# Strassen's seven products for the value half of an MLP up-projection, in a two-layer encoder kernel on one core

## The chip, the cores and the metric

The kernel runs on one core of a Trainium2 chip. The metric is device time in microseconds (us), from the program's start to its end on that core; lower is better. Three runs of the kernel before gave 2897.88, 2903.08 and 2912.84 us, a median of 2903.08 us.

## The reference, cut to what matters

Two layers over 640 tokens: 512 of a prompt and 8 requests of 16 new tokens each. All data is float32. A layer ends with a gated MLP, whose gate half goes through a causal convolution of width 3 (per sequence):

```python
x = x + jnp.sum(g * proj, axis=2) @ w_out
u = _rms(x, norm_ffn_g) @ ffn_w_up              # 1024 -> 2 * 2816
a_up, v_up = u[..., :D_FF], u[..., D_FF:]       # gate half, value half
ext = jnp.concatenate([conv0.astype(a_up.dtype), a_up], axis=1)
c = ffn_conv_b + sum(ext[:, j:j + T] * ffn_conv_w[j] for j in range(CONV_W))
x = x + (jax.nn.silu(c) * v_up) @ ffn_w_down    # 2816 -> 1024
```

## The kernel before, in words

Everything is one program of some 48,500 instructions. A framework places the instructions on the engines' queues: it goes by the order of the source, but lets an instruction pass an earlier one of its engine that isn't ready yet in its own model of time. The order on each queue is then fixed; on the chip each queue runs strictly in that order and waits where an operand or a buffer isn't there. A buffer belongs to a tag with so many copies (`wh`: 3, `wl`: 3, `mm`: 2, `sc`: 3, ...); a new tile of a tag waits until the users of the oldest one are done.

TensorE multiplies in the format fp32r, which keeps less than float32. So each matrix is split into a high part (a cast on ACT, line 98, in `split`) and a low part, the rest (a subtraction on DVE, line 99), and each product is three matmuls: high by high, high by low, low by high. `wload` brings a weight block from DRAM into `wr` and splits it into `wh` and `wl`.

The stages of a layer: the attention and recurrence branches with their gates; the mix of the branches (lines 1120 to 1149); the output projection with the residual (line 1160 on); the up-projection with the gated activation (lines 1193 to 1249); the down-projection (lines 1274 to 1300).

**Output projection.** Four units of 256 columns, in each five token tiles of 128. In the last unit (`u == 3`) `norm_tile(t - LAG)` is called two tiles later: squares on ACT, the root on POOL (line 127), scaling on DVE (line 144), four transposes per half on TensorE, then the split of the transposed tile into high and low (lines 98, 99, 151, 153). Its result is `xh`, `xl`: the normalised activations, features by tokens.

**Up-projection.** Eleven units `u` of 256 of the 2816 columns. A unit first does the gate half: two blocks of 128 columns times two halves of the 640 tokens (`HT` = 320), each a group of 8 x 3 = 24 matmuls of 320 columns into one PSUM bank `mm` (`projB`, matmuls at line 123). ACT copies the sums out (lines 1206 to 1209), DVE does the convolution (lines 1220 to 1222), ACT the tanh (line 1226), DVE the product that makes it SiLU (line 1227). Then the value half: again four groups of 24, into the banks `sc`, and DVE multiplies them with the gate (lines 1244 to 1247) into `mid`, which stays in SBUF. So a unit has 96 + 96 matmuls.

**Down-projection.** For each half `s` of the 1024 output columns, eleven steps `kp` take two blocks of `mid`, split them on ACT and DVE into `hl` (five buffers `ob`), split a weight block, and run 2 x 3 matmuls of 512 columns for each of the five token tiles (`down`, lines 1270 to 1272). The last three steps are kept back (`late`), so that the token tiles end one after the other.

Of the kernel before, what the change touches and what calls it, by code (L numbers as in the profile page):

```python
# [18 lines left out]
D = 1024  # L19
SEQ = 512  # L20
NB = 8
NS = 16
# [8 lines left out]
class Cols:  # L31
    """tiles [128, n], one a block, read as one [128, k, n]."""
# [21 lines left out]
def body(ctx: ExitStack, tc: tile.TileContext, i, o, depth=DEPTH):  # L54
    nc = tc.nc
    V, A, G, PE, SY = nc.vector, nc.scalar, nc.gpsimd, nc.tensor, nc.sync
    pool = ctx.enter_context(tc.tile_pool(name="sb", bufs=1))
    pp = ctx.enter_context(tc.tile_pool(name="ps", bufs=1, space=PSUM))
    dp = ctx.enter_context(tc.tile_pool(name="dr", bufs=1, space=DRAM))
    BUFS = {  # L60
# [3 lines left out]
    }  # L64
    BUFS.update(TUNE)
    cnt = [0]

    def T(tag, shape, dt=F32, bufs=None):
        cnt[0] += 1
        return pool.tile(shape, dt, tag=tag, bufs=bufs or BUFS[tag], name=f"{tag}_{cnt[0]}")  # L70

    def P(tag, shape=(128, 512)):
        cnt[0] += 1
        return pp.tile(list(shape), F32, tag=tag, bufs=BUFS[tag], name=f"{tag}_{cnt[0]}")

    def C(name, shape, dt=F32, bufs=1):
        cnt[0] += 1
        return pool.tile(shape, dt, tag=name, bufs=bufs, name=f"{name}_{cnt[0]}")
# [50 lines left out]
    def norm_T(xs, gsrc, xh, xl, stag="st"):  # L129
        """rms of token-major halves xs[h] [128, NT, 512] -> split transposed xh, xl, each [128, 4, TOK] x2; a tile a call."""  # L130
# [30 lines left out]
    def projB(w, c0, xh, xl, evac, tag="mm", hs=(0, 1)):  # L161
        """feature-major: columns c0..c0+128 of the unit, all tokens in two halves."""
# [21 lines left out]
    def tok_out(l, t, name, ap_fn):  # L184
        """DMA a token tile: prompt rows or sample rows."""

    def constants():
# [16 lines left out]
        Sbd = []  # L204
        for k in range(4):
            s_ = C(f"Sbd{k}", [128, 128])
            G.memset(s_[:], 0.0)
            Sbd.append(s_)

        qz = []  # L210
        for c in range(2):
            z_ = C(f"qz{c}", [128, 2, TOK])
            G.memset(z_[:], 0.0)
            qz.append(z_)

        # hgrn lower bound: softmax over depth, running sum less the first
# [27 lines left out]
        return masks, rope, hsel, bsel, half2, identf, Sbd, qz, lbs, lb1  # L244

    wz0 = []
    for l in range(depth):
# [15 lines left out]
        # ---- input norm  # L263
# [36 lines left out]
        def scaled_rstd(v, n, rs):  # L300
            """rstd of v / rs^2 over 64, times 1 / rs (rs in its first n columns, the next n are scratch)."""
# [41 lines left out]
        def stream_a():  # L343
# [48 lines left out]
            def a_latents(t):  # L392
# [13 lines left out]
                # rotary key  # L406
# [7 lines left out]
                # queries  # L414
# [19 lines left out]
            for t in range(NT):  # L434
# [5 lines left out]
                for hf in range(2):  # L440
# [21 lines left out]
                    else:  # L462
# [4 lines left out]
                        for bq in range(2):  # L467
                            # rows: high, low, high
# [26 lines left out]
            # == A keys and values  # L495
# [48 lines left out]
            # == A prompt attention  # L544
# [28 lines left out]
            # == A sample requests, against the latent rows  # L573
# [81 lines left out]
        # ---- branch C: differential attention  # L655
        def stream_c():
# [21 lines left out]
            def c_inproj(u):  # L678
                """queries and keys of two blocks; high and low parts of the prompt's go to DRAM."""
# [44 lines left out]
            def c_stack(blk, hh):  # L724
                """a head's two queries and keys as 96 rows: high, low, high against high, high, low."""
# [11 lines left out]
            # == C prompt attention  # L737
# [4 lines left out]
            def p_probs(un, q):  # L742
                """a head's weights for a block of queries, over the first softmax's scale."""
# [59 lines left out]
            # == C sample requests  # L803
# [69 lines left out]
            for bh in range(2):  # L873
# [8 lines left out]
                # each row holds two heads' values; its own half counts  # L882
# [22 lines left out]
        # ---- branch B: gated recurrence  # L905
        def stream_b():
            ob = kept["ob"] = T("ob", [128, 4, TOK])
            late = None
            for u in range(2):
# [39 lines left out]
                for c in range(2):  # L949
# [5 lines left out]
                    # == B diagonal and levels  # L955
# [18 lines left out]
                    # qz holds each head's q (zero in the other head's rows) with its decay from the start of its block, k that to the end of its block, F a block's whole decay  # L974
# [32 lines left out]
                    # == B chunks  # L1007
# [45 lines left out]
                    # == B sample states  # L1053
# [30 lines left out]
        # the branches and gates are traced interleaved, each string's letter advancing its own  # L1084
# [3 lines left out]
        if l == 0:  # L1088
            masks, rope, hsel, bsel, half2, identf, Sbd, qz, lbs, lb1 = constants()
# [20 lines left out]
        ob = kept["ob"]  # L1110

        # == mix: branch projections under their gates
# [38 lines left out]
        # ---- output projection and residual  # L1151
        x2 = [T("ob", [128, NT, 512]) for _ in range(2)]
        for h in range(2):
            if l == 0:
                SY.dma_start(x2[h][:, 0:4], i["x_prompt"][0, :, h * 512:(h + 1) * 512].rearrange("(t p) d -> p t d", p=128))
# [227 lines left out]
```

## Time and profile before

| | |
|---|---|
| median of three runs | 2903.08 us (2897.88 to 2912.84) |
| the profiled execution: first to last instruction (its span) | 2904.4 us |
| its own time as a run | not given apart; the span is 1.3 us above the median and inside the range of the runs |
| TensorE matmuls busy | 2835.3 us, 98% of the span, 19,600 matmuls |
| DVE, ACT, POOL busy | 1472.6, 987.4 and 352.5 us |
| data moved | 293.66 MB, 101 GB/s in the mean |
| stretch of the up-projection in layer 0 and in layer 1 | about 980 to 1304 us, about 2433 to 2738 us |

A matmul's own duration in this profile overlaps with the next one's, so the step from one start to the next is what a matmul costs. "Idle before" an instruction is charged to what came last of the things it waited for.

### The profile page before, as it was taken

To read this page: it belongs to the slowest core of one execution; us is meant where nothing else is said; L and a number is where in the kernel's file an instruction comes from. 1 tells how busy PE (TensorE), PEld (TensorE's weight loads), DVE (VectorE), ACT (ScalarE), POOL (GpSimd) and SP (SyncE) were. 2 spreads that over 40 slices of the span, in tenths; PEclk is the share of its full clock that TensorE was granted. 3 is DMA by queue.
4 is the path that set the end of the run, shared out by engine and by line. 5 is a ranking of instruction groups with operands and counts; after the bars stand their busy time and mean duration, and the time that the engine had idled before them with its cause. 6 is when DMAs were issued, how large, how long until landed. Compare 5 with 4: busy or idle time off the path is not lost. (4 is left out here: it accounts for less than half of the span.)

```text
span 2904.4 us, 48551 instructions
## 1 busy us (share of the span) xinstructions
PE 2835.3 (98%) x19600; PEld 2542.7 (88%) x19600; DVE 1472.6 (51%) x3117; ACT 987.4 (34%) x2074; POOL 352.5 (12%) x559
## 2 busy tenths in 40 slices
PE   7999999999999999999999999999999999999998
PEld 7979997778889999998899799977788899999976
DVE  5465464355565544443454654633646545444444
ACT  4444453232221322222444443623222223222332
POOL 1000120012122001000000011200222210110000
PEclk9999999999999999999999999999999999999999
DMA  4213563322244222222333136443232442222222
GB/s 147 69 50 110 169 173 115 118 89 82 80 140 155 74 73 73 73 85 76 98 110 93 41 120 184 122 141 116 82 98 66 154 134 70 73 77 81 86 73 73
DMA packets 297996, 293.66 MB, mean 101 GB/s; under 512 B 51493, under 2 KB 254765, under 8 KB 296237
## 3 DMA queue, kind: packets, MB, share of 16 engines
q1 hardware_dynamic: 290092, 277.97, 31.1%
q0 software_dynamic: 7680, 12.59, 1.8%
q8 instruction: 155, 2.54, 0.4%
q14 instruction: 69, 0.56, 0.1%
HBM read 245.37 MB, written 44.09 MB: 100 GB/s over the span
## 5 line engine op out<-in xcount | busy, mean ns | idle before, releaser
L99 DVE TENSOR_TENSOR wl<-wr,wh 128x1024 fp32r<-128x1024 f32 (+2 forms) x292 | 370.6, 1270 | 339.1 <-ACT wh L98 336.3
L98 ACT CAST wh<-wr 128x1024 fp32r<-128x1024 f32 (+2 forms) x292 | 305.1, 1045 | 605.9 <-PE sc L123 213.0
L123 PE MATMUL mm<-xh,wh 128*128 128x320 f32 x1280 | 409.0, 320 | 0.0
L123 PE MATMUL mm<-xl,wh 128*128 128x320 f32 x1280 | 408.1, 319 | 0.0
L123 PE MATMUL mm<-xh,wl 128*128 128x320 f32 x1280 | 405.2, 317 | 0.0
L123 PE MATMUL sc<-ob,wh 128*128 128x320 f32 x1568 | 400.6, 310 | 2.9 <-DVE pd L1142 2.9
L123 PE MATMUL mm<-wh,xh 128*128 128x256 f32 (+1 forms) x960 | 281.2, 293 | 6.6 <-ACT xh L1148 3.9
L123 PE MATMUL mm<-wh,xl 128*128 128x256 f32 (+1 forms) x960 | 280.4, 292 | 1.1 <-DVE xl L99 1.0
L123 PE MATMUL mm<-wl,xh 128*128 128x256 f32 (+1 forms) x960 | 280.8, 293 | 0.0
L123 PEld LDWEIGHTS sc<-ob,wh 128*128 128x128 f32 x1568 | 275.1, 188 | 3.7 <-DVE pd L1142 3.7
L123 PE MATMUL mm<-ob,wh 128*128 128x320 f32 (+1 forms) x1088 | 275.1, 312 | 1.2 <-ACT ob L98 0.6
L123 PE MATMUL sc<-ob,wl 128*128 128x320 f32 x832 | 257.6, 310 | 0.0
L123 PEld LDWEIGHTS mm<-xh,wh 128*128 128x128 f32 x1280 | 243.0, 190 | 7.2 <-issue 3.1
L123 PEld LDWEIGHTS mm<-xh,wl 128*128 128x128 f32 x1280 | 242.6, 190 | 6.3 <-issue 3.4
L123 PEld LDWEIGHTS mm<-xl,wh 128*128 128x128 f32 x1280 | 242.9, 190 | 4.9 <-issue 0.4
L123 PE MATMUL mm<-ob,wl 128*128 128x320 f32 (+1 forms) x720 | 224.7, 312 | 0.0
L123 PE MATMUL sc<-pd,wh 128*128 128x320 f32 x608 | 189.3, 311 | 3.4 <-DVE pd L1142 3.4
L123 PEld LDWEIGHTS mm<-wh,xh 128*128 128x128 f32 x960 | 184.1, 192 | 9.3 <-ACT xh L1148 4.3
L123 PEld LDWEIGHTS mm<-ob,wh 128*128 128x128 f32 x1088 | 189.4, 188 | 2.9 <-DVE ob L99 1.1
L123 PEld LDWEIGHTS mm<-wh,xl 128*128 128x128 f32 x960 | 183.8, 192 | 1.7 <-DVE xl L99 1.2
L123 PEld LDWEIGHTS mm<-wl,xh 128*128 128x128 f32 x960 | 184.1, 192 | 1.1 <-issue 0.8
L123 PEld LDWEIGHTS sc<-ob,wl 128*128 128x128 f32 x832 | 156.2, 188 | 0.0
(379 smaller groups left out, 5218.3 us busy)
## 6 DMA issues: line engine op xcount, KB each, us to landing
wr<-in_w_in_dram SPq DMA_DIRECT2D x104, 512.0 KB, 4.2
wr<-in_ffn_w_up_dram SPq DMA_DIRECT2D x88, 512.0 KB, 3.6
wr<-in_ffn_w_down_dram SPq DMA_DIRECT2D x44, 512.0 KB, 3.6
pd<-in_cache_diff_k_dram SPq DMA_DIRECT2D x64, 256.0 KB, 3.8
pd<-in_cache_diff_v_dram SPq DMA_DIRECT2D x64, 256.0 KB, 3.2
gp<-g SPq DMA_DIRECT2D x48, 320.0 KB, 3.8
pd<-gp SPq DMA_DIRECT2D x48, 320.0 KB, 3.8
wr<-in_w_branch_dram SPq DMA_DIRECT2D x24, 512.0 KB, 3.6
```

What stands on the lines that cost most here:

```text
L98: a = A.copy(hi, src)
L99: v = V.tensor_tensor(lo, src, hi.bitcast(F32), op=ALU.subtract)
L123: PE.matmul(out, lhsT=a, rhs=b, start=(j == 0), stop=(j == n - 1))
```

## The change

**SBUF by stage.** Before, one pool holds all tiles. After, a small fixed pool keeps `xh`, `xl`, `wr`, `wh`, `wl` and small things, and each stage opens pools of its own on the left or right side of SBUF and closes them at its end; a tile that lands on the bytes of an earlier stage's tile waits for the users of that tile alone. The scratch of the branches (`qz`, `Sbd` and others) is cleared again in each layer.

**Residual.** `x2`, the residual, is loaded ahead of the mix, written to DRAM tile by tile in the last unit of the output projection, and read back at the start of the down-projection (2 x 1280 KB).

**Activations.** `norm_tile` splits each transposed tile into `aq` (four quadrants: two halves of the tokens by two halves of the features) and also copies it whole into `raw`. `norm_sums` then forms the four sums of quadrants that Strassen's scheme needs and splits them into `S`.

**Value half.** Four products of quadrants (96 matmuls) are replaced by seven products of 4 x 3 = 12 matmuls of 320 columns, 84 in all. Weight sums are made on DVE in the raw block and split as before. Sums that several outputs share stay in a PSUM bank, in which the next product goes on accumulating; three of them are copied to SBUF by ACT and added to another bank by DVE.

**Order.** The gate groups of unit `u + 1` are written between the products of unit `u`.

**Gate.** As before, 96 matmuls; the halving of SiLU is folded into the convolution's weights.

**Gated activations.** Each block goes to DRAM (`midp`, 22 x 320 KB a layer) and comes back twice in the down-projection, once for each `s` (11 x 640 KB each time). `hl` has three buffers in place of five.

The diff, cut to its core:

```diff
+        mr = Phase("mr", "right", aq=4, wr8=2, wh2=2, wl2=2, cw=1, cvo=1, rows=1)
+        nr = Phase("nr", "right", raw=1, e=2, t=2)
...
+    def wslot(shape):
+        wring[0] += 1
+        more = "2" if wring[0] % 5 > 2 else ""
+        return T("wh" + more, shape, F32R), T("wl" + more, shape, F32R)
+    def st_weights(src, c0):
+        w = src.rearrange("(k p) n -> p k n", p=128)
+        raw = T("wr8", [128, 8, 256])
+        for u in range(2):
+            SY.dma_start(raw[:, 4 * u:4 * u + 4], w[:, 4 * u:4 * u + 4, c0:c0 + 256])
...
+        b1h, b1l = wslot([128, 8, 128])
+        split(b1h[:], b1l[:], raw[:, :, 0:128])
+        b2h, b2l = wslot([128, 4, 128])
+        split(b2h[:], b2l[:], b(1, 1))
+        V.tensor_tensor(b(0, 0), b(0, 1), b(0, 0), op=ALU.subtract)
+        V.tensor_tensor(b(0, 1), b(1, 1), b(0, 1), op=ALU.subtract)
+        V.tensor_tensor(b(1, 1), b(1, 1), b(0, 0), op=ALU.subtract)
+        V.tensor_tensor(b(1, 0), b(1, 0), b(1, 1), op=ALU.subtract)
+        t0h, t0l = wslot([128, 4, 256])
+        split(t0h[:], t0l[:], raw[:, 0:4])
+        t1h, t1l = wslot([128, 4, 256])
+        split(t1h[:], t1l[:], raw[:, 4:8])
...
+        def prod(j):
+            z = {1: "X", 6: "X", 7: "X", 4: "X", 5: "Y", 3: "Y", 2: "Z"}[j]
+            first = j in (1, 5, 2)
+            if first:
+                bank[z] = P({"X": "sc", "Y": "tp", "Z": "sc"}[z])[:, :HT]
...
+            prs = [pr for k in range(sh.shape[1]) for pr in ((th[:, k], sh[:, k]), (th[:, k], sl[:, k]), (tl[:, k], sh[:, k]))]
+            for q, (a, b) in enumerate(prs):
+                PE.matmul(ps, lhsT=a, rhs=b, start=first and q == 0, stop=q == len(prs) - 1, skip_group_check=not first)
+            if j in (1, 5, 6):
+                kept_[j] = copy_of(ps)
+            elif j == 2:
+                out(0, 0, kept_[1], ps)
+            elif j == 3:
+                out(0, 1, kept_[6], ps)
+            elif j == 7:
+                out(1, 1, kept_[5], ps)
+            else:
+                out(1, 0, None, ps)
...
+        def norm_sums(c0, c1, S):
+            def r(h, u):
+                return raw[:, 4 * u:4 * u + 4, h * HT + c0:h * HT + c1]
+            V.tensor_tensor(r(1, 1), r(1, 0), r(1, 1), op=ALU.add)
+            G.tensor_tensor(r(1, 0), r(0, 0), r(1, 0), op=ALU.subtract)
+            split(S[0][:, 0, :, c0:c1], S[0][:, 1, :, c0:c1], r(1, 1))
+            V.tensor_tensor(r(0, 0), r(1, 1), r(0, 0), op=ALU.subtract)
+            V.tensor_tensor(r(0, 1), r(0, 1), r(0, 0), op=ALU.subtract)
+            split(S[1][:, 0, :, c0:c1], S[1][:, 1, :, c0:c1], r(0, 0))
+            split(S[3][:, 0, :, c0:c1], S[3][:, 1, :, c0:c1], r(0, 1))
+            split(S[2][:, 0, :, c0:c1], S[2][:, 1, :, c0:c1], r(1, 0))
...
+        norm_tile(3)
+        norm_sums(0, 512 - HT, S)
+        norm_tile(4)
+        norm_sums(512 - HT, HT, S)
...
+            def out(h, c, s, ps):
+                v = ps
+                if s is not None:
+                    v = T("m", [128, HT])
+                    V.tensor_tensor(v[:], s, ps, op=ALU.add)
...
+        ops = {1: plain[0], 2: plain[1], 3: sums[3], 4: plain[3], 5: sums[0], 6: sums[1], 7: sums[2]}
...
+        for u in range(NU):
+            gates = gate_unit(u + 1, ccs[u + 1]) if u + 1 < NU else iter(())
+            value = value_unit(u, ccs[u], wv)
+            for step in (1, 5, 2, 6, 3, 0, 7, 0, 4, 0, 0):
+                if step:
+                    value(step)
+                else:
+                    next(gates, None)
+                if step == 6 and u + 1 < NU:
+                    wv = st_weights(up, FF + (u + 1) * 256)
...
-                hl = T("ob", [128, 4, TOK], F32R)
+                hl = T("hl2" if (11 * s + kp) % 3 else "hl", [128, 4, TOK], F32R)
+                mid = T("pd" if s or kp else "m0", [128, 2, TOK])
+                SY.dma_start(mid[:], midp[kp])
```

In the value loop a `0` stands for one gate group of 24 matmuls of the next unit. The gate half's weights use `wh` and `wl` too (two tiles a unit); `wslot` gives three of five tiles of the value half to `wh` and two of five to the new `wh2`. The value outputs use `m` (2 buffers), the copies `s` (4).

## Rows read from the trace of the kernel before

**Rows 1.** The page: its head and part 1 (busy us, share, instructions).

```profile
span 2904.4 us, 48551 instructions
...
PE 2835.3 (98%) x19600; PEld 2542.7 (88%) x19600; DVE 1472.6 (51%) x3117; ACT 987.4 (34%) x2074; POOL 352.5 (12%) x559
```

**Rows 2.** Stretches: up-projection of layer 1, down-projection of layer 0 (columns head it).

```profile
core 0: us, PE busy (x) PEld busy (x) DVE busy (x) ACT busy (x) POOL busy (x), PEclk, DMA share, GB/s
2433.00:2738.00 305.00, 305.00 (x2077) 305.00 (x2076) 140.94 (x201) 80.67 (x134) 30.82 (x84) 1.00 0.24 75
1304.00:1453.00 149.00, 149.00 (x647) 119.46 (x646) 66.92 (x85) 54.49 (x83) 1.10 (x2) 1.00 0.27 85
```

**Rows 3.** The chain that ended last: one gate and one value half of 21.

```profile
2512.24 14.12 PE mm L123 x96
2526.36 14.12 PE sc L123 x96
```

**Rows 4.** Groups by line, 2445 to 2730 us: busy us, mean ns, idle before.

```profile
L99 DVE TENSOR_TENSOR wl<-wr,wh 128x1024 fp32r<-128x1024 f32 x40 | 49.0, 1224 | 23.3 <-ACT wh L98 22.5
L98 ACT CAST wh<-wr 128x1024 fp32r<-128x1024 f32 x40 | 42.1, 1053 | 81.6 <-PE sc L123 69.9 <-issue 11.7
L1222 DVE SCALAR_TENSOR_TENSOR a<-e,pd,a 128x656 f32<-128x656 f32 x21 | 18.8, 896 | 0.4
...
L1227 DVE SCALAR_TENSOR_TENSOR a<-e,a 128x656 f32<-128x656 f32 x20 | 16.8, 839 | 8.2 <-ACT e L1226 8.2
...
L1220 DVE TENSOR_SCALAR a<-e,pd 128x656 f32<-128x656 f32 x20 | 12.7, 636 | 89.8 <-POOL pd L1223 89.8
...
L1244 DVE SCALAR_TENSOR_TENSOR pd<-a,sc 128x320 f32<-128x320 f32 x5 | 2.4, 479 | 6.0 <-PE sc L123 6.0
...
L1246 DVE SCALAR_TENSOR_TENSOR pd<-a,sc 128x192 f32<-128x192 f32 x4 | 1.4, 352 | 0.4 <-PE sc L123 0.4
L1247 DVE SCALAR_TENSOR_TENSOR pd<-a,sc 128x128 f32<-128x128 f32 x4 | 1.1, 280 | 0.0
```

**Rows 5.** Groups by line, one shape each, whole span: nearest shapes on DVE.

```profile
L95 DVE COPY a<-tp 128x512 f32<-128x512 f32 x62 | 42.7, 689 | 66.2 <-PE tp L831 46.3 <-PE tp L857 13.6 <-PE tp L562 5.1
...
L99 DVE TENSOR_TENSOR ob<-xh,ob 128x640 fp32r<-128x640 f32 x32 | 25.0, 818 | 3.8 <-ACT ob L98 3.8
...
L99 DVE TENSOR_TENSOR pd<-tp,pd 128x512 fp32r<-128x512 f32 x32 | 21.9, 690 | 10.3 <-ACT pd L98 10.3
```

**Rows 6.** Stretches: the entry to the up-projection in layer 1.

```profile
2415.00:2430.00 15.00, 14.39 (x115) 13.83 (x115) 13.97 (x37) 8.29 (x17) 2.02 (x5) 1.00 0.12 36
2430.00:2445.00 15.00, 15.00 (x105) 14.83 (x104) 9.65 (x19) 5.64 (x11) 3.51 (x9) 1.00 0.20 62
```

**Rows 7.** Timeline there: low parts of tiles 3 and 4 (DVE), first gate copies (ACT).

```profile
2429.61 0.87 DVE L153 TENSOR_TENSOR pd<-tp,ob 128x128 fp32r<-128x128 f32 x4
...
2434.11 0.88 DVE L153 TENSOR_TENSOR pd<-tp,ob 128x128 fp32r<-128x128 f32 x4
...
2430.39 0.43 ACT L1206 COPY e<-mm 128x320 f32<-128x320 f32 x1 [0.83 <-PE mm L123]
...
2438.29 0.32 ACT L1208 COPY e<-mm 128x192 f32<-128x192 f32 x1 [3.10 <-PE mm L123]
```

**Rows 8.** Timeline in the mix of layer 1: a POOL addition beside DVE.

```profile
2333.53 2.43 DVE L99 TENSOR_TENSOR wl<-wr,wh 128x1024 fp32r<-128x1024 f32 x1 [0.45 <-ACT wh L98]
...
2333.31 1.56 POOL L1145 TENSOR_TENSOR pd<-pd,pd 128x640 f32<-128x640 f32 x1 [1.96 <-DVE pd L1142]
```

**Rows 9.** Stretches: a wait between mix and output projection, and after it.

```profile
928.00:932.00 4.00, 2.25 (x20) 2.04 (x18) 1.89 (x3) 1.32 (x2) 2.60 (x1) 1.00 0.18 59
932.00:936.00 4.00, 3.78 (x19) 3.79 (x20) 1.25 (x2) 0.16 (x1) 0.00 (x0) 0.57 0.21 72
```

**Rows 10.** DMA issues: KB each, median us from issue to landing.

```profile
wr<-in_ffn_w_down_dram SPq DMA_DIRECT2D x44, 512.0 KB, 3.6
...
ob<-op SPq DMA_DIRECT2D x4, 1280.0 KB, 6.9
```

More of the change, by code (lines that the diff above doesn't have):

```diff
@@ L1088, in body @@
         if l == 0:
-            masks, rope, hsel, bsel, half2, identf, Sbd, qz, lbs, lb1 = constants()
+            masks, rope, hsel, bsel, half2, identf, lbs, lb1 = constants()
+        Sbd = []
+        for k in range(4):
+            s_ = C(f"Sbd{k}", [128, 128])
+            G.memset(s_[:], 0.0)
+            Sbd.append(s_)
+        qz = []
+        for c in range(2):
+            z_ = C(f"qz{c}", [128, 2, TOK])
+            G.memset(z_[:], 0.0)
+            qz.append(z_)
         lam = C("lam", [128, 8])
@@ L1149, in body @@
                         V.scalar_tensor_tensor(ml[blk // 4][:, blk % 4], acc[c][:], 0.5, hi.bitcast(F32), op0=ALU.mult, op1=ALU.subtract)
[L1152 to L1158 removed]
+        ar.close()
@@ new lines, in body @@
+        mr = Phase("mr", "right", aq=4, wr8=2, wh2=2, wl2=2, cw=1, cvo=1, rows=1)
+        nr = Phase("nr", "right", raw=1, e=2, t=2)
+        x2park = [dp.tile([128, NT, 512], F32, name=f"x2park{l}_{h}", tag=f"x2p{l}{h}")[:] for h in range(2)]
+        raw = T("raw", [128, 8, TOK])
+        aq = [T("aq", [128, 2, 4, HT], F32R) for _ in range(4)]
+        gb = [T("e", [128, 512]) for _ in range(2)]
+        for h in range(2):
+            SY.dma_start(gb[h][:], i["norm_ffn_g"][l][h * 512:(h + 1) * 512].partition_broadcast(128))
@@ new lines, in norm_tile @@
+        def norm_tile(t):
+            st = S1()
+            cs = slice(t * 128, (t + 1) * 128)
+            for u in range(2):
+                A.activation(raw[:, 4 * u:4 * u + 4, cs], x2[u][:, t].rearrange("p (k n) -> p k n", k=4), AF.Square, accum_out=st[:, u:u + 1])
+            V.tensor_tensor(st[:, 2:3], st[:, 0:1], st[:, 1:2], op=ALU.add)
+            rstd(st[:, 3:4], st[:, 2:3], D)
+            for u in range(2):
+                xn = T("t", [128, 512])
+                V.scalar_tensor_tensor(xn[:], x2[u][:, t], st[:, 3:4], gb[u][:], op0=ALU.mult, op1=ALU.mult)
+                ps = P("tp")
+                for k in range(4):
+                    PE.transpose(ps[:, k * 128:(k + 1) * 128], xn[:, k * 128:(k + 1) * 128], ident[:])
+                pv = ps[:].rearrange("p (k n) -> p k n", k=4)
+                for h in range(2):
+                    lo_, hi_ = max(t * 128, h * HT), min((t + 1) * 128, (h + 1) * HT)
+                    if lo_ < hi_:
+                        q = aq[2 * h + u]
+                        src = pv[:, :, lo_ - t * 128:hi_ - t * 128]
+                        split(q[:, 0, :, lo_ - h * HT:hi_ - h * HT], q[:, 1, :, lo_ - h * HT:hi_ - h * HT], src)
+                copy(raw[:, 4 * u:4 * u + 4, cs], pv)
@@ L1159, in body @@
         for u in range(4):
             w = wload2(i["w_out"][l], u * 256)
-            if u == 3:
-                xh, xl = [wide("ob"), wide("ob")], [wide("ob"), Cols([T("pd", [128, TOK], F32R) for _ in range(4)])]
-                norm_tile = norm_T(x2, i["norm_ffn_g"][l], xh, xl)
             for t in range(NT):
@@ L1187, in body @@
             PE.transpose(tp[:, g * 128:g * 128 + n], rows[:n, g], ident[:n, :n])
-        copy(cw[:].rearrange("p j f -> p (j f)"), tp[:, :20 * NF])
-        cvo = T("pd", [128, 18, NF])
-        mid = []
+        V.tensor_copy(cw[:, 0:16].rearrange("p j f -> p (j f)"), tp[:, :16 * NF])
+        A.activation(cw[:, 16:20].rearrange("p j f -> p (j f)"), tp[:, 16 * NF:20 * NF], AF.Copy, scale=0.5)
+        cvo = T("cvo", [128, 18, NF])
+        midp = [dp.tile([128, 2, TOK], F32, name=f"mid{l}_{u}", tag=f"mid{l}_{u}")[:] for u in range(NF // 2)]
```

200 lines of the change are left out of this document (121 added, 79 removed), and 3 rows, old and new, of the table BUFS.

## The prediction

> **What bounds the kernel now.** The page first: matmuls are busy 98% of the span, DVE 51%, ACT 34% [rows 1]. Shares are averages, so next the stretches: in the up-projection of layer 1 TensorE is busy for 305.00 of 305 us at the full clock, DVE for 46%, ACT for 26%; the down-projection is as dense [rows 2]. The chain of waits says the same in another way: through the up-projection it runs over matmuls alone, 96 of them in 14.12 us, one half after the other [rows 3]. One matmul of 320 columns so costs 14.12 / 96 = 0.1471 us, a unit of 192 costs 28.24 us, and nothing else ends a wait there. A matmul taken away is time won, for as long as the other engines keep up.
>
> **What is removed.** Seven products of 12 are 84 matmuls for 96: 12 x 0.1471 = 1.765 us a unit, 22 units in two layers: **-38.8 us**. A unit then has 180 matmuls, 26.48 us. Those that stay keep their shape (320 columns, fp32r), so I take the old step; this term has no range of its own.
>
> **DVE and ACT in the steady state.** DVE before, in a unit: four low parts of 1.224, two convolutions of 0.636 + 0.896 + 0.896 + 0.839 = 3.27, and 2 x (0.479 + 0.352 + 0.280) of output products, 13.7 us [rows 4]; the stretch shows 140.94 / 305 x 28.24 = 13.0. After: two gate low parts (2.45), value low parts 3 x 1.224 + 0.69 = 4.36, four subtractions of 512 elements at 0.69 (2.76, priced by the 512-element row of [rows 5]), the convolutions (6.53), three additions of 0.479 and the output products (3.66): 19.8 us, 75% of 26.48. ACT gains three copies of 0.43 [rows 7] and half a cast: about 10 us of 26.48. TensorE remains the longest engine. New waits stand in its queue: product 6 waits for ACT's copy of product 1 (0.43 us, under products 5 and 2, 3.5 us), product 4 for DVE's addition after 7 (0.48 us, under a gate group of 3.5 us). Behind each stand the next unit's gate groups, but the covers are seven times the work and more, and while they last I price this at **0**. If DVE is inside a convolution when asked, 3.27 us is what the cover has to take, just under 3.5. Bounds: 0 to 1 us a unit within this case, 20 us; what lies beyond is the second rival.
>
> **The entry.** Here the cover is thin. Before, DVE is busy for 13.97 + 9.65 of the 30 us around the entry, so 6.4 us are free, while TensorE passes from one stage to the next with 0.6 us lost [rows 6]. The last token tile's low parts end at 2434.99, the first gate group that needs it is copied out at 2438.29: 3.3 us of room [rows 7]. The change adds to DVE there, for each layer: half of the ten copies into `raw`, 5 x 0.69 = 3.4, less 5 x 0.18 for the four-piece low parts that become one (0.87 to 0.69), and 0.3 for tile 2, cut at token 320: 2.8 us. `norm_sums`: three additions and four low parts each at 768 and 512 elements; the rows at 512 and 640 (0.690, 0.818) give 0.94 and 0.69, so 7 x 1.63 = 11.4 us. And POOL's subtraction in it reads SBUF beside DVE: in the mix a DVE low part that overlaps POOL's addition of 640 elements (1.56 us) took 2.43 us where it takes 1.22 otherwise [rows 4, 8], so I count POOL's time against DVE, 1.56 x (768 + 512) / 640 = 3.1 us. Together 17.3 us. Of these 6.4 go into the free time, and 3.5 lie under products 1 and 2, which need only unsummed operands of the first token half: 7.4 us remain. A wait of TensorE also costs clock: after the 2.1 us without matmuls before 932.2, four microseconds were granted 0.57, one level of 1.2 GHz for most of it, 4 x 0.43 = 1.7 us lost [rows 9]. With one such fall, 9.1 us a layer, **+18.2**. From below: 3 us a layer, if the work left over hides after 2445, where DVE was under half busy; from above: all 17.3 and two falls, 20.7 a layer. I take the middle because the free time is DVE's own in these very rows.
>
> The Trainium skill (SBUF — State Buffer, Who interferes with whom) makes the POOL row a rule: the pair of ports that the two share is locked for a whole instruction, and a DVE instruction with two SBUF inputs is held up by a GpSimd one that reads SBUF. By it the 3.1 us are certain; if DVE were not held at all the sum would be 6.2 us lower.
>
> **The exit.** Gated activations now pass through DRAM. Before, the down-projection moved 85 GB/s at a DMA share of 0.27 [rows 2]; 11 x 640 KB in 75 us add about 95 GB/s, a share near 0.6, with four buffers ahead of use. A step of 30 matmuls lasts 149 / (647 / 30) = 6.9 us, a landing of 512 KB 3.6 us, of 1280 KB 6.9 us [rows 2, 10]. SP issues the two loads of `x2` first; step 1's block queues behind up to 13.8 us of them and its split (about 1.5 us) behind that, while step 0 covers 6.9 us and the loads may start up to 7 us before the last product ends. I put it at 1 us a layer (0 to 8). With three `hl` for five, the first step of the second half can split only when the kept-back steps free a buffer, 2.8 us before their end: 0.5 us a layer (0 to 2). **+3**.
>
> **Edits at nothing.** Storing `x2` and `mid`: SP only, no one waits. Clearing `qz` and `Sbd` again: POOL, idle most of the time [rows 1]. Pools by stage: a first tile may wait for an old user of its bytes; no row shows one, the nearest are the boundaries of [rows 2, 6], dense; -3 to +8 us.
>
> **Sum.** -38.8 + 0 + 18.2 + 3 = -17.6 against the span of 2904.4: 2886.8. The median is 1.3 lower: **2885 us**, 0.6% faster. Ends of this case: entry 6, nothing else, 2870; above that line up to 2889.
>
> **Rivals.**
> *The entry eats the gain.* The sums of tiles 0 to 3 are written ahead of `norm_tile(4)`, and DVE takes them in order: tile 4 then ends not at 2435 but 2.8 + 6.6 us later, the first value weights (low parts, 4.4, subtractions, 2.8) come after the convolution of unit 0, and TensorE, with only unit 0 to do, waits two or three times. Price: the upper bound, 2 x 20.7 + 3 - 38.8 = +5.6, so **2909 us**, no change that can be told. For it: DVE at 93% in the first of [rows 6]. Against: the framework may pass a blocked instruction, and ten transposes leave DVE holes there.
> *Weight buffers become the bound: slower.* A unit needs six split weight tiles, in three `wh` and two `wh2`, and the next unit's gate pair is written behind the four value tiles. In two of five ring positions three value tiles sit in `wh`: then the gate pair can't be split until the products that free them are done. Chain of such a unit: gate groups end, a value tile is split (1.05 + 1.22), four products (7.06), the gate tile is split (2.3), four gate groups (14.12): 25.8 us, just under 26.48. If each low part stands behind a convolution's three steps (2.43) on DVE, 30.6, so 4.2 us over, in 22 x 2/5 = 9 units: +37, **2922 us**. It decides from 1.5 us a unit in the mean on. For it: DVE at 75% where before it was 46%; before, the same kind of chain (four tiles through three buffers) had DVE free when asked. Against: the first products of the unit after fill such a wait, and their tiles are in `wh2`.
> *The change doesn't do what it says* is no rival: the matmuls can be counted in the loops.
>
> **How the numbers follow.** A measurement of this kernel tells 0.5% (14.5 us) from no change: faster is below 2888.6, slower above 2917.6. The first case 0.45, the entry 0.30, the weight buffers 0.25. The range reaches from the low end of the first to the middle of the last, 2868 to 2922; the first case alone 2870 to 2889.
>
> **What would show it.** Right: 84 value matmuls a unit at 0.147 us apart; units of 26.5 us; one or two holes of TensorE before the second unit, 5 to 10 us a layer, with DVE busy through them and the granted clock down after each; none later. Entry rival: holes of 15 us and more, DVE full until `S` is written. Buffer rival: TensorE idle in every few units, released by `wh` casts or low parts. The forecast is wrong if TensorE's busy share within the units falls under 97%, or if the down-projection waits for `mid`.

## The result, and the profile after

The changed kernel takes **2954.4 us** (median of 4 runs, 2948.95 to 2956.36) where the kernel before took 2902.4 in the same set: a ratio of **1.0165, 95% interval 1.0139 to 1.0191**. It is slower by 1.7%, 69 us above the forecast of 2885 and above its range (2868 to 2922).

The head of the page and its part 1, after; it answers to [rows 1]:

```profile
span 2954.5 us, 48746 instructions
...
PE 2824.8 (96%) x19336; PEld 2511.0 (85%) x19336; DVE 1620.7 (55%) x3328; ACT 1066.6 (36%) x2215; POOL 350.2 (12%) x569
```

264 matmuls are gone, as the change says (19,600 to 19,336), and yet the span grew by 50.1 us. TensorE's busy share fell from 98% to 96%: it waits more. To see where, both traces are cut at the same instructions (the merge after each branch projection, the residual's addition after the output projection, the gate's first eviction, the first matmul of the down-projection, its last addition). Times in us, layer 0 / layer 1:

| stretch | before | after | difference |
|---|---|---|---|
| start of the layer to the first merge in the mix | 845.2 / 814.1 | 851.9 / 826.0 | +6.7 / +11.9 |
| rest of the mix and output projection | 145.6 / 147.8 | 147.0 / 146.5 | +1.4 / -1.3 |
| last addition of the residual to the first gate eviction (entry) | 6.3 / 6.3 | 22.8 / 23.6 | +16.5 / +17.3 |
| rest of the up-projection | 307.6 / 307.6 | 293.6 / 292.7 | -14.0 / -14.9 |
| down-projection | 157.4 / 155.1 | 171.5 / 167.7 | +14.1 / +12.6 |

The sum is +50.3. So each of the boundaries lost something, and the up-projection gained less than 19.4 us a layer. Each column is one execution, and the first row is the least certain: over the thirteen traces with the new pools that stretch takes 839 to 852 us in layer 0. The next rows show the four places one by one.

**Within the units.** Stretches after; columns as in [rows 2]:

```profile
1045.00:1300.00 255.00, 250.58 (x1673) 245.16 (x1673) 172.40 (x252) 94.43 (x159) 19.93 (x72) 1.00 0.31 101
...
2510.00:2760.00 250.00, 245.47 (x1639) 240.03 (x1638) 164.33 (x239) 90.36 (x154) 19.67 (x72) 1.00 0.30 97
1345.00:1480.00 135.00, 135.00 (x582) 108.28 (x582) 58.42 (x74) 46.69 (x71) 1.57 (x3) 1.00 0.47 153
```

Before, TensorE was busy for 305 of 305 us [rows 2]. Now 255 us hold 1673 matmuls, 0.1524 us each for 0.1471, so 8.9 us more than they took before; it is the same in layer 1. From start to start, the loss lies in 46 steps of more than 0.165 us, most of them where a group of matmuls begins; the others stay at 0.147. The longest waits come together, some 2 us around 1112 us and again around 1249 us, five units later. DVE is at 68%, so it has room. What releases TensorE there (its longer waits from 1045 to 1300 us: how long, how often, the longest):

```profile
PE mm L137 <- ACT wh L112: 2.1, 2, 1.0
PE sc L254 <- ACT wh L112: 1.2, 2, 0.6
PE mm L137 <- DVE wl L113: 0.8, 2, 0.4
```

All are weights being split. In the first fence, the last of the three stretches is the body of the down-projection: dense, so the round trip through DRAM doesn't slow it as a whole.

**The entry.** Timeline of layer 0 (start, duration, engine, instruction, idle time before it and what ended it); TensorE's row, then DVE's, then the gate's first eviction on ACT, and two stretches:

```profile
1022.89 0.64 PE L254 MATMUL sc<-aq,wl 128*128 128x320 f32 x1 [8.69 <-DVE wl L113]
...
1014.98 0.94 DVE L113 TENSOR_TENSOR xl<-raw,xl 128x768 fp32r<-128x768 f32 x1
...
1020.41 0.69 DVE L1284 TENSOR_TENSOR raw<-raw 128x512 f32<-128x512 f32 x1
1021.02 0.69 DVE L113 TENSOR_TENSOR xl<-raw,xl 128x512 fp32r<-128x512 f32 x1
1021.62 1.22 DVE L113 TENSOR_TENSOR wl<-wr,wh 128x1024 fp32r<-128x1024 f32 x1
...
1021.66 0.42 ACT L1353 COPY e<-mm 128x320 f32<-128x320 f32 x1
...
1005.00:1015.00 10.00, 7.30 (x37) 6.34 (x35) 9.70 (x14) 5.16 (x9) 1.84 (x1) 0.83 0.01 2
1015.00:1025.00 10.00, 2.11 (x8) 2.11 (x9) 8.81 (x14) 4.23 (x9) 4.36 (x7) 0.70 0.00 1
```

The low part of the first value weight is the last DVE row (`wl`). It is what product 1 still needs, and it stands in DVE's order behind nearly all of `norm_sums`; ACT's eviction of the gate stands behind the sums' casts in the same way. TensorE idles for 8.7 us (3.8 in layer 1, where the low part got ahead of most of the second group of sums). Its granted clock falls twice, to 0.83 and 0.70 in the two stretches.

**The exit.** Timeline of SP's queue, the activations' cast on ACT, TensorE's next row, then five stretches, and one in the same hole of layer 1:

```profile
1321.60 1.01 SPq L1422 DMA_DIRECT2D out_dram<-rows  x1
1322.70 0.80 SPq L1430 DMA_DIRECT2D x<-x2park  x2
1323.56 12.20 SPq L1446 DMA_DIRECT2D pd<-mid  x5
...
1333.09 1.35 ACT L112 CAST hl<-pd 128x640 fp32r<-128x640 f32 x2 [7.41 <-DMA pd<-mid]
...
1333.86 1.22 PE L1436 MATMUL mm<-wh,hl 128*128 128x512 f32 x2 [9.09 <-ACT hl L112]
...
1320.00:1330.00 10.00, 4.78 (x21) 3.42 (x20) 1.77 (x4) 1.30 (x2) 0.00 (x0) 0.98 0.96 366
1326.00:1332.00 6.00, 0.00 (x0) 0.00 (x0) 0.93 (x1) 0.00 (x0) 0.00 (x0) 0.80 1.00 422
1330.00:1340.00 10.00, 6.14 (x15) 4.68 (x16) 4.63 (x6) 4.06 (x6) 0.00 (x0) 0.51 0.94 364
1334.00:1340.00 6.00, 6.00 (x15) 4.54 (x16) 4.47 (x6) 3.15 (x5) 0.00 (x0) 0.52 0.90 332
1340.00:1350.00 10.00, 10.00 (x45) 8.03 (x44) 2.69 (x3) 2.31 (x3) 0.00 (x0) 1.00 0.69 244
...
2785.00:2790.00 5.00, 0.00 (x0) 0.00 (x0) 0.42 (x1) 0.00 (x0) 0.00 (x0) 0.70 1.01 424
```

Step 0 of the down-projection ends at 1324.8. SP issues the residual's 2.56 MB at 1322.70, right behind the last store of the up stage, and step 1's activations right behind those; SP's own waits name none for these reads, so it is the place in the queue that makes them late. The DMA engines are then full (share 0.96 and 0.94) at 366 and 364 GB/s, which moves 2.56 + 0.64 MB in about 9 us; the cast starts at 1333.09. From 1330 to 1340 us TensorE was granted 0.51, nearly all of it the lower of its two levels. For the first 3.9 us of these it still waits; behind the wait 15 matmuls take 6.0 us, 0.40 each where the next 45 take 0.22, so the clock costs another 2.7 us. The Trainium skill (DMA: Bandwidth & Descriptors, Specifications) gives two limits, some 358 GB/s for a core's share of HBM and 435 for the ports into SBUF. The two stretches of ten microseconds lie near the first; inside the hole both layers lie above it, near the second: 422 from 1326 to 1332 us, and 424 in layer 1.

**Ahead of the mix.** SP's queue, the merge on DVE and TensorE's next row, in layer 0; then the first gate read, the merge and TensorE's row in the kernel before:

```profile
838.73 0.37 SPq L1198 DMA_DIRECT2D x<-in_x_prompt_dram  x1
842.64 0.34 SPq L404 DMA_DIRECT2D gp<-g  x1
843.04 0.43 SPq L1199 DMA_DIRECT2D x<-in_x_sample_dram  x1
843.57 0.39 SPq L1198 DMA_DIRECT2D x<-in_x_prompt_dram  x1
844.01 0.56 SPq L1199 DMA_DIRECT2D x<-in_x_sample_dram  x1
844.62 0.42 SPq L1229 DMA_DIRECT2D pd<-gp  x1
...
851.89 0.88 DVE L1233 SCALAR_TENSOR_TENSOR pd<-pd,sc 128x320 f32<-128x320 f32 x2 [3.27 <-DMA pd<-gp]
852.43 0.90 PE L137 MATMUL sc<-ob,wh 128*128 128x320 f32 x2 [5.70 <-DVE pd L1233]
...
840.78 0.43 SPq L1138 DMA_DIRECT2D pd<-gp  x1
...
845.17 0.88 DVE L1142 SCALAR_TENSOR_TENSOR pd<-pd,sc 128x320 f32<-128x320 f32 x2
...
845.70 0.56 PE L123 MATMUL sc<-ob,wh 128*128 128x320 f32 x2 [1.21 <-DVE pd L1142]
```

The residual's loads now precede the mix in the program, and they were issued ahead of the first gate read (`pd<-gp`); the merge of the first branch waits for that read and starts 7.3 us after its issue; before, it was 4.4. Meanwhile the banks of `sc` stay full, and TensorE waits 5.7 us (8.2 in layer 1) where it waited 1.2 at this place before.

### The profile page after: what moved, and what is told of

It is laid out like the page before. It is cut to its first block, busy times and chain, and to the rows that moved or that the text cites. A ratio compares the mean times of both kernels' runs of the same rounds, so it can differ in the third digit from the quotient of the medians.

```text
span 2954.5 us, 48746 instructions
## 1 busy us (share of the span) xinstructions
PE 2824.8 (96%) x19336; PEld 2511.0 (85%) x19336; DVE 1620.7 (55%) x3328; ACT 1066.6 (36%) x2215; POOL 350.2 (12%) x569
## 5 line engine op out<-in xcount | busy, mean ns | idle before, releaser
L113 DVE TENSOR_TENSOR wl<-wr,wh 128x1024 fp32r<-128x1024 f32 (+2 forms) x336 | 412.3, 1231 | 341.3 <-ACT wh L112 339.9
L112 ACT CAST wh<-wr 128x1024 fp32r<-128x1024 f32 (+2 forms) x336 | 340.3, 1018 | 579.4 <-PE mm L137 179.8
L137 PE MATMUL mm<-aq,wh 128*128 128x320 f32 x1408 | 314.3, 313 | 6.0 <-ACT wh L112 4.1
L137 PEld LDWEIGHTS mm<-aq,wh 128*128 128x128 f32 x1408 | 236.1, 190 | 13.3 <-ACT wh L112 9.7
L137 PE MATMUL mm<-aq,wl 128*128 128x320 f32 x704 | 214.6, 311 | 1.6 <-DVE wl L113 1.6
L137 PE MATMUL sc<-ob,wh 128*128 128x320 f32 x512 | 139.2, 316 | 14.3 <-DVE pd L1233 14.3
L137 PEld LDWEIGHTS mm<-aq,wl 128*128 128x128 f32 x704 | 132.3, 189 | 3.5 <-DVE wl L113 3.5
L141 POOL TENSOR_TENSOR st<-st,mhalf 128x1 f32<-128x1 f32 (+3 forms) x53 | 56.1, 1059 | 646.5 <-DVE st L140 606.1
L254 PE MATMUL sc<-aq,wh 128*128 128x320 f32 x528 | 119.2, 311 | 0.0
L107 ACT COPY a<-tp 128x512 f32<-128x512 f32 (+3 forms) x100 | 47.4, 474 | 166.8 <-PE tp L903 61.4
```

Of the source, the lines that this page charges most:

```text
L107: A.copy(dst, src)
L112: a = A.copy(hi, src)
L113: v = V.tensor_tensor(lo, src, hi.bitcast(F32), op=ALU.subtract)
L137: PE.matmul(out, lhsT=a, rhs=b, start=(j == 0), stop=(j == n - 1))
L141: G.tensor_tensor(r, r, mhalf[:, :r.shape[-1]], op=ALU.pow)
L254: PE.matmul(ps, lhsT=a, rhs=b, start=first and q == 0, stop=q == len(prs) - 1, skip_group_check=not first)
```

## The experiments

Four causes are thus named: the units, the entry, the exit and the loads ahead of the mix. All runs are edits of the changed kernel, and each was timed beside runs of the kernel before. Gains are differences of ratios times 2904 us, against 1.0165; intervals of single ratios are about 0.0015 to 0.0035 wide on either side, 4 to 10 us, so a gain under some 10 us isn't told from nothing by the times alone.

**Is it the layout or the products?** The value half plain, in the new layout:

```
-            return st_unit(w, ops, out)
+            for c in range(2):
+                for h in range(2):
+                    mm3(ps, ...)
+                    out(h, c, None, ps)
...
-        norm_sums(...)
```

> The value half is computed plainly (96 matmuls a unit, no sums, weights split as the gate's), in the order of the kernel before, while the pools by stage, the residual's two moves and the round trip of the gated activations through DRAM stay. Theory, most of the loss is the layout's: mix + 12, exit + 27, some + 4 in the branches, so 2903 + 43 = about 2946, and the seven products in this layout are worth about + 8 beside it. Rival, the layout is nearly free and the seven products bring the loss: 2903 to 2912.

Measured: 2947.8 us, ratio 1.0136 (1.0115 to 1.0156). The layout alone makes the kernel 1.4% slower, as the theory said; the rival falls. With the losses of the layout in place, the seven products bring another 0.3%, 8 us (the two intervals overlap), in place of -38.8.

**The exit, first try.**

```
-        for h in range(2):
-            SY.dma_start(x2[h][:], x2park[h])
...
                 mid = T("pd" if s or kp else "m0", [128, 2, TOK])
+                if kp == 6:
+                    SY.dma_start(x2[s][:], x2park[s])
```

> The re-read of the residual, 2.56 MB, is issued in step 6 of each half of the down-projection (x2's first half in the first, its second half in the second) and no longer ahead of the reads of the gated activations. Theory, the exit queue: the holes of 9.2 and 10.4 us ahead of the second step of the down-projection shrink to under 2 us, the half-clock stretches of 10.2 us behind them go, and the kernel gains 2 x (9.8 + 5.1) = about 27 us less a rest of some 3: 2926 to 2932. Rival, the round trip through DRAM slows the whole down-projection whatever the order: the holes move to a later step and the gain is under 8 us, 2946 to 2954.

Measured: 2942.1 us, ratio 1.0118 (1.0086 to 1.0151), a gain of 14 us, about half. The hole shrank to 3.4 us (3.8 in layer 1) and did not go: of the four activation reads that start together, the first still took 4.6 us from its issue to the cast that reads it.

**The exit, second try.** As above, and a second early buffer in bytes that the up stage does not use:

```
-        hp = Phase("hp", "left", hl=1, m0=1)
+        hp = Phase("hp", "left", hl=1, m0=2)
...
-                mid = T("pd" if s or kp else "m0", [128, 2, TOK])
+                mid = T("pd" if s or kp > 1 else "m0", [128, 2, TOK])
```

> The residual's re-read in step 6 as in the first run, and a second read buffer of gated activations outside the bytes of the up stage, so that steps 0 and 1 of the down-projection are both read early (13.8 us of matmuls instead of 6.9 before the first read that has to wait for bytes). Theory, what was left of the hole (3.6 and 4.0 us) is the first read that waits for bytes and shares the queues with three more: holes under 1 us, another 8 to 12 us gained with the half clock behind them: 2930 to 2935. Rival, the queues are full either way and the hole moves to step 2: 2940 to 2944, as the first run.

Measured: 2934.8 us, ratio 1.0101 (1.0073 to 1.0130), a gain of 19 us. Stretch across the exit in this run:

```profile
1312.00:1342.00 30.00, 28.42 (x122) 22.27 (x121) 12.64 (x17) 12.00 (x17) 0.00 (x0) 1.00 0.85 312
```

TensorE is busy for 28.4 of 30 us and keeps the full clock, with the DMA engines as busy as before (0.85). The down-projection takes 161.5 and 157.6 us, from 171.5 and 167.7, still 4.1 and 2.5 more than in the kernel before; TensorE's wait here, 1.6 us, is a part of that, and the rest was not traced. So it was the order of the transfers and too little read ahead, not their sum. (That the reads had to wait for bytes, as the text above supposes, the trace doesn't show: they stand behind the up stage's last stores.)

**Ahead of the mix, first try.** The loads moved to the second and third quarter of the mix:

```
...
         for u in range(4):
+            if u in (1, 2):
+                SY.dma_start(x2[u - 1]..., ...)
```

> The two loads of the residual, issued ahead of the mix stage, are issued at its second and third quarter. Theory, the gate reads queue behind the residual: the holes of 5.9 and 8.3 us ahead of the mix (matmul into sc released by the merge of pd) and the half clock behind them go down to what the kernel before has there (about 2 us a layer) and the kernel gains 10 to 14 us: 2940 to 2944. Rival, the stage's own first reads saturate the queues by themselves: a gain of 0 to 4 us, 2950 to 2954.

Measured: 2952.1 us, ratio 1.0154 (1.0134 to 1.0173), a gain of 3 us. This decided nothing: the queue's order is not the program's. In the trace one load was issued at 831.6, ahead of every gate read, and the other at 841.9, ahead of the third.

**Ahead of the mix, second try.** The same edit with each load held behind what the program has put on SP's queue by then:

```
-                SY.dma_start(x2[u - 1]..., ...)
+                tc.keep_in_program_order(SY.dma_start(x2[u - 1]..., ...))
```

> As the run before it that moved the residual's loads to the second and third quarter of the mix, but now held in their place in SP's queue (there they were issued early again, one of them ahead of the gate reads). Theory, the gate reads queue behind the residual: the holes ahead of the mix fall to some 2 us a layer or less and the kernel gains 8 to 12 us against the kernel with the change: 2942 to 2946. Rival, the mix's own first reads (gates, parked branches, weights) saturate the queues: 0 to 4 us, 2950 to 2954.

Measured: 2944.6 us, ratio 1.0134 (1.0100 to 1.0167), a gain of 9 us, as the theory said, though the times alone don't tell it from nothing. The traces do: the holes ahead of the mix fell from 5.7 and 8.2 us to 1.2 and 2.6. In all seven traces with the loads in the changed kernel's place, the holes are 5.0 to 5.8 and 7.0 to 8.4 us; in all five that hold them back, 1.2 and 2.6. The first load is now issued at 856, behind six gate reads.

**The price of the sums.** Sums and the copies that feed them left out:

```
-                copy(raw[:, 4 * u:4 * u + 4, cs], pv)
...
-        S = [T(tag, [128, 2, 4, HT], F32R) for tag in ("xh", "xl", "xh", "xl")]
+        S = [aq[q] for q in (0, 1, 2, 3)]
...
-        norm_sums(...)
```

> Left out: the sums of activations (norm_sums) and the plain copies that feed them; products 3, 5, 6 and 7 read plain activation tiles in place of sums. The count of matmuls is that of the kernel with the change. Theory, the vector engine's backlog at the entry: the hole of 8.9 us (first layer) and 3.9 us (second) ahead of the first product shrinks to under 2 us, the two or three half-clock stretches at each entry shrink with it, and the kernel gains 20 to 28 us: 2926 to 2934. Rival, the first product's weights are late by their own load and split: the holes stay, and the gain is under 6 us.

Measured: 2928.6 us, ratio 1.0069 (1.0049 to 1.0090), a gain of 28 us, at the upper end. The hole ahead of the first product is gone in both layers (the entry takes 9.1 and 9.0 us for 22.8 and 23.6). The sums and their copies are what makes the first value weights late.

**The sums behind gate 1.**

```
-        norm_sums(0, 512 - HT, S)
...
-            for step in (1, 5, 2, 6, 3, 0, 7, 0, 4, 0, 0):
+            for step in (1, 5, 2, 6, 3, 0, 7, 0, 4, 0, 0) if u else (1, 2, 0, 9, 0, 0, 0, 5, 6, 3, 7, 4):
+                if step == 9:
+                    norm_sums(0, 512 - HT, S)
+                    norm_sums(512 - HT, HT, S)
...
```

> Nothing left out: in the first unit of a layer the order is gate 0, products 1 and 2, the four steps of gate 1, then products 5, 6, 3, 7, 4, and the sums of activations are traced behind the first step of gate 1 (their source tile lies on the other side of SBUF for that), so that the first product's weights no longer queue behind them on the vector engine. Theory, the vector engine's backlog: 17 us of sums are covered by 17.6 us of matmuls that need none of them, the holes of 8.9 and 3.9 us go, and the kernel gains 18 to 24 us of the 26 that leaving the sums out gave: 2930 to 2936. Rival, the sums' own work stays in the way wherever it stands (the scalar engine's evictions queue behind the sums' casts): under 8 us, 2946 to 2954.

Measured: 2957.5 us, ratio 1.0175 (1.0145 to 1.0205): nothing gained. TensorE's row there, the cast of the weight tile that it needs, and DVE's rows ahead of it:

```profile
1020.02 0.64 PE L137 MATMUL mm<-aq,wl 128*128 128x320 f32 x1 [5.97 <-DVE wl L113]
...
1011.92 1.07 ACT L112 CAST wh<-wr 128x1024 fp32r<-128x1024 f32 x1
...
1016.47 1.21 DVE L113 TENSOR_TENSOR wl<-wr,wh 128x1024 fp32r<-128x1024 f32 x1
1017.60 0.82 DVE L1365 SCALAR_TENSOR_TENSOR a<-e,a 128x656 f32<-128x656 f32 x1
1018.35 0.47 DVE L1381 TENSOR_TENSOR md<-a,m 128x320 f32<-128x320 f32 x1
1018.76 2.34 DVE L113 TENSOR_TENSOR wl<-wr,wh 128x1024 fp32r<-128x1024 f32 x2
```

The hole moved from product 1 to the next gate group (`mm`). It ends with the low part of gate 1's first weight tile, the first of the two in DVE's last row (from 1018.76). The tile's high part was there at 1012.99, and no buffer held its low part back: that stood in DVE's order behind weight subtractions, another split and the convolution's work. The second tile did wait for a buffer, since products 1 and 2 read `b1` out of it; its cast starts at 1013.92, behind their last matmul at 1012.83, but it isn't what ends this wait. The edit gave the sums a cover, and the cover's own weights queued on the engine that the sums fill. The theory's place was right and the remedy was not. Of the two, the rival is nearer: the work on DVE stays in the way.

**Mix, exit and this entry together.** The three edits above in one kernel.

> The three edits together: residual's loads held behind the gate reads of the mix's first quarter, two early read buffers and the late re-read at the exit, the sums behind the first gate step. Theory, the three boundaries add: 10 + 21 + 21 = 52 us off 2954, 2897 to 2908, level with the kernel before; the seven products' 38.8 us are then still eaten by the ring of weight buffers and small steps within the units (18 us) and by the rests of the boundaries. Rival, the boundaries share one cause (queues and clock) and the gains overlap: 2915 to 2930.

Measured: 2921.1 us, ratio 1.0055 (1.0034 to 1.0076), a gain of 32 us: mix and exit add (9 + 19), the entry adds next to nothing. The number lies in the rival's range, but not by the rival's cause: what overlaps is not the boundaries' gains; one of the three edits was empty by itself.

**The turn of the weight buffers.** The five pairs of buffers in one turn, so that each comes again five splits later:

```
     def wslot(shape):
-        wring[0] += 1
         more = "2" if wring[0] % 5 > 2 else ""
+        wring[0] += 1
...
-            w = [wload(...) for v in range(2)]
...
+            for v in range(2):
...
+                w.append(wslot([128, 4, 256]))
+                split(w[v][0][:], w[v][1][:], raw_[:])
...
-                if step == 6 and u + 1 < NU:
+                if step == 7 and u + 1 < NU:
                     wv = st_weights(up, FF + (u + 1) * 256)
```

> The kernel with the change, with one edit: the five pairs of weight buffers are used in one turn (gate, gate, b1, b2, t0, t1), and the next unit's value weights are traced behind product 7 and not behind product 6. Sums, mix and exit stay as they are. Theory, the weight buffers' turn costs the 9.3 and 9.8 us lost within the units of the two layers (lumps of 2.5 us in every fifth unit and a rest spread over the others): the units become dense and the kernel gains 16 to 20 us against 2954: 2934 to 2939. Rival, the units lose to the vector engine's load (68% busy there) and the turn is no matter: 0 to 5 us.

Measured: 2928.9 us, ratio 1.0102 (1.0067 to 1.0137), a gain of 18 us (25 by the medians of the two sets). The stretch that held 1673 matmuls:

```profile
1045.00:1300.00 255.00, 255.00 (x1741) 255.00 (x1740) 182.29 (x261) 102.05 (x169) 24.76 (x78) 1.00 0.30 100
```

1741 matmuls now, 0.1465 us each, no idle time, and DVE busier than before (71%). In the trace the up-projections of both layers, with their entries, are 23 us shorter together. So the units lost to the order in which buffers were handed out, not to DVE's load. The edit also writes the next unit's value weights one product later; the run doesn't separate the two.

**All four.** Mix, exit and turn as above; in the first unit of a layer half of gate 1's weights are split ahead of gate 0, and `b1`, `b2` into buffers that are free before the up stage:

```
+        w0 = [gate_half(0, v) for v in range(2)]
+        w1 = [gate_half(1, 0)]
+        for _ in gate_unit(0, ccs[0], w0):
+            pass
+        st = st_weights(up, FF)
+        wv = next(st)
+        w1.append(gate_half(1, 1))
```

> The three edits together, and the five pairs of weight buffers used in one turn (gate, gate, b1, b2, t0, t1; each buffer comes again five splits later) in place of gates on three of them alone; the first unit splits b1 and b2 into buffers that are free before the up stage, takes half of gate 1's weights ahead of gate 0, and has its sums behind gate 1's first step. Theory: in the run before, the entry's hole only moved from the first product to gate 1, whose weights waited for b1's buffer and then for the vector engine; with buffers of its own the entry loses under 6 us a layer instead of 14 to 18, and the lumps of 2.5 us at every fifth unit go: 2921 - 20 - 8 = 2893, between 2885 and 2902, level with or under the kernel before (2907). Rival, the vector engine is the entry's bound wherever the sums stand (some 30 us of work between the first gate and product 5): 2910 to 2921.

Measured: **2881.6 us**, ratio **0.9925 (0.9910 to 0.9940)**, faster than the kernel before by 0.75% and below the theory's range. Stretches of this run, the last three at the entry of layer 0:

```profile
1045.00:1290.00 245.00, 245.00 (x1671) 244.74 (x1670) 174.99 (x255) 95.55 (x157) 22.57 (x70) 1.00 0.32 108
...
990.00:1005.00 15.00, 14.49 (x104) 13.50 (x103) 14.72 (x29) 9.88 (x21) 1.36 (x4) 1.00 0.25 80
1005.00:1020.00 15.00, 13.20 (x81) 12.93 (x80) 15.00 (x17) 8.23 (x14) 9.15 (x10) 0.90 0.04 11
1020.00:1035.00 15.00, 15.00 (x103) 15.00 (x102) 13.98 (x20) 6.60 (x13) 5.49 (x8) 0.99 0.17 47
```

DVE is busy for 43.7 of 45 us around the entry, so it is still the full engine there, but TensorE has work that does not ask for it: 2.3 us idle in 45.

**All but the entry, and the plain value half mended.** Two runs close the sum. The first has mix, exit and turn mended and the sums ahead of the first gate again; the second has the plain value half with mix and exit mended.

> The best kernel so far (2882) without its mended entry: mix, exit and the turn of the weight buffers mended, the sums again ahead of the first gate as in the change. Theory, the terms add: 2882 plus the entry's 20 us = 2898 to 2906, within 10 us of the kernel before. Rival, with weight buffers of their own the first products no longer wait behind the sums, and the order of the first unit is worth little: 2882 to 2890.

> The plain value half in the layout of the change (as in the fourth run), with the mix and the exit mended as in the run with all three edits. No sums, no seven products. Theory, the layout costs nothing of its own beyond those two queues: 2948 - 10 - 20 = 2918, less what the half clock behind them took, so 2906 to 2918, within 12 us of the kernel before. Rival, the round trip and the pools cost at places that the holes don't show (down-projection slowed throughout, branches): 2920 to 2935.

Measured: 2896.4 us, ratio 0.9982 (0.9967 to 0.9997), and 2914.5 us, ratio 1.0037 (1.0020 to 1.0054): the first just under the theory's range, the second inside it. The entry is worth (0.9982 - 0.9925) x 2904 = 17 us. Mended, the seven products are worth (1.0037 - 0.9925) x 2904 = 33 us of the 38.8 that were counted, and the mended layout costs 11 us. In the traces most of that lies in the second layer's branches, ahead of the mix: 822 to 834 us in every kernel with the new pools, 814.1 in the one trace of the kernel before. What causes it was not tried and stays open.

| kernel | us | ratio to before |
|---|---|---|
| changed kernel | 2954.4 | 1.0165 |
| mix mended | 2944.6 | 1.0134 |
| exit mended | 2934.8 | 1.0101 |
| turn of the weight buffers mended | 2928.9 | 1.0102 |
| mix, exit and turn | 2896.4 | 0.9982 |
| mix, exit, turn and entry | 2881.6 | 0.9925 |

The four gains, 9 + 19 + 18 + 17 = 63 us, make up most of the 70 us between the changed kernel and the last.

## Why the prediction was wrong

**What is removed: right.** 264 matmuls are gone and a step costs 0.1465 to 0.147 us where nothing waits. In the mended layout the products give 33 us of the 38.8.

**The exit: the step that failed most.** It was put at +3 and measured +26.7 (14.1 and 12.6). The price of the transfers was not too low: 13.8 us of loads were allowed ahead of step 1, and its block was there 10.4 us after their issue (1322.70 to 1333.09). What failed is the cover, "the loads may start up to 7 us before the last product ends". They started at 1322.70, some five microseconds after the last product's end and two before step 0's, because SP had the up stage's last stores, which wait for DVE and ACT, ahead of them. So 2 us were covered where 6.9 + 7 were counted. The clock's fall (2.7 us in layer 0) was not counted at the exit at all, though [rows 9] had shown one. The bound of 8 a layer was too low by 5 to 6.

**The steady state: priced at nothing, and at the upper end of its bound.** Priced at 0, bound 20; measured about 18 (two stretches of 8.9, and 18 by the run with the turn mended). The second rival had the mechanism, weight tiles that wait for a buffer, but it priced a rare long wait of 4.2 us in 9 units and set its threshold at 1.5 us a unit. What came was some 2 us in every fifth unit and short waits in the others, 0.8 a unit in the mean, within the first case's bound. DVE's load, which that part of the prediction weighed at length, was not the matter; it came out at 68% for the 75% forecast.

**The entry: nearly right.** Forecast 9.1 us a layer. The two rows of the table give 16.5 + 17.3 - 14.0 - 14.9 = +4.9; with the matmuls' -38.8 and the units' 18 taken out, 25.7 is left, 12.8 a layer (10.5 with the 23 us that the trace of the mended turn gives the units). The mechanism is the one named (sums on DVE ahead of the first value weights); the single durations were met (0.94 and 0.69 us for the sums). The clock fell twice where one fall was counted. POOL's share was too high: 1.6 us where 3.1 were counted (the rows are at the end). The rival "the entry eats the gain" named the place too, but the loss stayed below its price of 20.7.

**"Edits at nothing": missed a step.** The residual's loads ahead of the mix were not priced at all. They were part of the pools by stage, bounded by -3 to +8; the stretch up to the first merge grew by 18.6 between the two traces. The run that holds them back is 9 us faster; the rest remains in it, most of it in the branches of layer 1, and its cause is open.

**The numbers.** The misses were 24 (exit), 18 (units), 19 (ahead of the mix) and 7 (entry), 68 in all, and none went the other way. The forecast needed all four boundaries to hide their work at once; each was argued by itself, and the chances treated the two rivals as exclusive, where both occurred in part, together with two that had no rival. Of the two signs of being wrong that were named beforehand, one came: the down-projection waits for `mid`. The other did not, since the busy share within the units is 98% where under 97% was asked; the step of 0.1524 us for 0.1471 shows the loss that the share hides.

## What to carry to other kernels

A dense matmul stage turns removed matmuls into time only if what is moved to its edges is covered there: go through each boundary in SP's queue, and ask what must leave it ahead of the first read and what else is issued at that instant. Reads that are needed late (a residual) belong behind reads that are needed next, and that has to be held in the queue, since the order of issue need not be the program's. Where buffers are handed out in turn, write down for each whose reader must end first; one turn over all five, with the next weights written one product later, was worth 18 us here, and moving work under a cover was worth nothing while the cover's own weights queued on the engine that does this work.

## What the runs showed that was not expected

- A re-read of 2.56 MB held up 0.64 MB behind it for a wait of 9.1 us, with the DMA engines full, although the stage as a whole used under half of the DMA engines' time (share 0.47 from 1345 to 1480 us).
- The wait of 9.1 us at the exit came with a granted clock of 0.51 from 1330 to 1340 us. A wait of 1.6 us at the mended exit left it at 1.00, while one of 1.8 us at the entry of the fastest kernel came with 0.90 from 1005 to 1020 us. One of 2.3 us ahead of the mix, in the run that moved the loads without holding them, left it at 1.00 from 840 to 850 us. So the length of a single wait didn't tell what the clock did.
- POOL's subtractions beside DVE, in the entry of layer 0; timeline of POOL, then DVE, answering to [rows 8]:

```profile
1009.80 1.84 POOL L1281 TENSOR_TENSOR raw<-raw 128x768 f32<-128x768 f32 x1 [5.12 <-PE tp L1266]
1016.61 2.52 POOL L1281 TENSOR_TENSOR raw<-raw 128x512 f32<-128x512 f32 x1 [4.97 <-DVE raw L1280]
...
1011.07 1.38 DVE L113 TENSOR_TENSOR xh<-raw,xh 128x768 fp32r<-128x768 f32 x1
...
1019.16 0.71 DVE L1283 TENSOR_TENSOR raw<-raw 128x512 f32<-128x512 f32 x1 [1.16 <-POOL raw L1281]
```

The first subtraction held up one DVE low part (1.38 us, where its like took 0.94 at 1014.98). The second, a third smaller, took longer itself, while DVE's low parts beside it kept their time; DVE then waited 1.16 us for its result. So the loss falls on either of the two, and a sum that charges all of POOL's time to DVE, as the prediction did when it called the 3.1 us certain, is too high: 0.4 + 1.2 = 1.6 us.
